# Branch B's attention values with queries on partitions, and new weave numbers

## The chip, the cores and the metric

The kernel runs on one core of a Trainium2 chip. A core has a matrix engine (PE, with its weight loads shown apart as PEld), a vector engine (DVE), a scalar engine (ACT), a general engine (POOL) and a queue that issues transfers (SP). They work side by side, each in its own program order, and wait for each other by semaphores. The metric is the device time in microseconds of one execution.

## The reference, cut to what matters

One encoder layer is applied to two groups of 1024 tokens (`prompt`, then `sample`), all in float32. Branch B is differential attention with 4 heads; each head has two 64-wide query and key maps and 128-wide values:

```python
s = jnp.einsum('bqhmd,bkhmd->bhmqk', qblk, k).astype(jnp.float32) * scale
p = jax.nn.softmax(s, axis=-1)
pd = (p[:, :, 0] - lam * p[:, :, 1]).astype(v.dtype)
return jnp.einsum('bhqk,bkhe->bqhe', pd, v)
...
ob = diff_attention(qb, kb, vb, lam)
ob = rms_norm(ob, subln_g) * (1.0 - lam_init)
ob = ob.reshape(B, S, BR_B) * jax.nn.silu(zb)
```

So each query row of a head's 128 values is divided by its root mean square, scaled by a gain, and multiplied by a gate. Then both branches are projected (`w_proj_a`, `w_proj_b`), merged by sigmoid gates and projected again.

## The kernel before, in words

Everything is kept transposed: channels on partitions, tokens along the row. A large matmul splits each float32 operand into a high and a low part of a faster 32-bit type and adds three products (the input projection in `proj_tt` L613 and `z_gen` L824, the branch projections in `merge_gen` L1097, the output projection in `out_gen` L1128). The attention values are plain float32 matmuls; the profile shows two PE records for each such instruction of the code.

**Attention.** `attention` walks a list of units. In phases 0 and 1 these are branch A's; in phases 2 to 5 a unit is one head of branch B with a pair of 128-query tiles (`pr` 0 to 3), so there are 16 B units in a group and 32 in all. For each query tile and map, `softmax_unit` makes 128x1024 scores in a two-bank PSUM tile `s` (there are two of these), takes the row maximum on DVE, and the exponential on ACT into a tile `p`. `flip` adds the second map to the first (L895), transposes `p` in 32x32 blocks on DVE (L896), and four DMAs of 128 KB put the blocks in place in a tile `q`, keys on partitions (L901, `q<-p`). `b_values` then multiplies: the value block of 128 keys is the weight that PE holds, and 256 queries stream past it, eight instructions for a unit (L953). The result `acc` in the one PSUM tile `a` has the 128 value channels on partitions and the queries along the row. It is squared by ACT (L968), copied by DVE (L969) and stored to a DRAM tile `od`. Because the channels lie on partitions, the sum of squares of a query is a sum over partitions: two float32 matmuls against a column of ones (L975), with the squares as weights. DVE collects the sums (L977, `ssB`); after the last unit of a head POOL forms the inverse roots of all 1024 queries (L980 to L983).

**Back end.** `gated_gen(i, hf)` prepares the input of the projection for two heads (`i` 2 and 3 are branch B's pairs of heads) and one half `hf` of the queries (half 0 holds units `pr` 0 and 1, half 1 holds `pr` 2 and 3). On `hf` 0 of a B pair it first turns the roots of two heads by a PE transpose (L1041), copies the rows (L1043) and stores them to a DRAM tile `rB`. Then, for each head, it loads `od` and the gate `zd`, loads the roots spread over all 128 partitions (`tab<-rB`, L1063), multiplies the three (L1064, L1068) and splits the product in two parts (L1069, L1070) in a tile `u`, which `merge_gen` uses as a moving operand (L1097).

**Order.** `weave` interleaves the streams of a phase (attention, the next head's projections, the gates' projections) by tables of weights: `Z_SHARE`, `ATT_W`, `IN_A`, `Z_A` and so on. `LAST_ATT`, `LAST_FILL`, `GATED_A` and `TAIL` do it for the stretch in which the last head's attention runs beside branch A's merge. On top of that a list scheduler sets each engine's final program order, and inside `attention` work has a higher priority. PE, DVE, ACT and POOL then run that order as it stands.

Of the kernel before, what the change touches and what calls it, by code (L numbers as in the profile page):

```python
# [37 lines left out]
    (8, 21, 4, 2, 4, 3),  # L38
    (13, 12, 5, 3, 2, 6),
)  # L40
Z_HEAD = (7, 6)
Z_HEAD_A = (-0.3, -0.32)
ATT_W = (
    (0.825, 1.067, 1.068, 1.192, 1.03, 1.769),
    (1.154, 1.862, 1.041, 1.271, 0.783, 1.144),
)
IN_A = (
    (0.32, -0.07, 0.7, 0.05, 0.25, 0.15),
    (0.1, -0.05, 0.33, 0.3, -0.03, 0.55),
)  # L50
Z_A = (
    (0.2, 0.05, 0.12, -0.05, -0.1, -0.05),
    (0.03, 0.07, 0.2, 0.15, -0.3, -0.1),
)
LAST_ATT = (47, 41)
LAST_FILL = (22, 23)
GATED_A = (0.1, -0.15)
# [4 lines left out]
FIRST_ATT = 15  # L62
FIRST_A = 0.26
TAIL = (2, 5)
TAIL_A = (1.15, 1.2)
LAG = 2
Z_FIRST = (9, 8)
Z_FIRST_A = (-0.05, -0.05)
# [4 lines left out]
BEHIND_A = 1.4  # L73
AHEAD = 100
PV_LAG = 2
A_WAIT = 1
TRAIN = 200

WHOLE = (True, True)
# [31 lines left out]
def kernel(ctx: ExitStack, tc: tile.TileContext, t: dict):  # L111
# [669 lines left out]
    def vb_gen(ht, out, pr):  # L781
        w = load_w(w_cols(w_in, (C_VB + pr * 256, 256)))
        if WHOLE[pr]:
            v = utile().bitcast(F32).rearrange("p (n h e) -> p n h e", n=NTT, h=2)
            out[2 * pr], out[2 * pr + 1] = v[:, :, 0], v[:, :, 1]
        else:
            vs = [utile().rearrange("p (n s e) -> p n s e", n=NTT, s=2) for _ in range(2)]
            out[2 * pr], out[2 * pr + 1] = vs
        for tt in range(NTT):
            ps = yield from proj_tt(ht, w, tt)  # L790
            if WHOLE[pr]:
                nc.scalar.activation(v[:, tt].rearrange("p h e -> p (h e)"), ps, AF.Copy)
                yield 1
                continue
            for i in range(2):
                vp = ps[:, i * P : (i + 1) * P]
                nc.scalar.activation(vs[i][:, tt, 0, :], vp, AF.Copy)
                nc.vector.tensor_tensor(
                    out=vs[i][:, tt, 1, :], in0=vp, in1=vs[i][:, tt, 0, :].bitcast(F32), op=ALU.subtract
                )  # L800
            yield 1
# [35 lines left out]
    def query_order(x):  # L837

        return x.rearrange("p (t i b) -> p i t b", t=2, i=4)

    def piece_order(x):
        return x.rearrange("p (i t b) -> p i t b", t=2, i=4)

    def softmax_unit(q, rs, sw, k, pt, su):


        m = tiny.tile([P, 1], F32, tag="m", name=nm("m"))
        s = sbank()
        for n in range(2):
            sl = slice(n * 512, (n + 1) * 512)  # L850
            nc.tensor.matmul(s[:, sl], q, k[:, sl], start=True, stop=False)  # L851
            nc.tensor.matmul(s[:, sl], sw, k[:, sl], start=False, stop=True)  # L852
        nc.vector.tensor_reduce(out=m, in_=s, axis=AX.X, op=ALU.max, negate=True)  # L853
        nc.scalar.activation(m, m, AF.Copy, scale=rs)
        nc.scalar.activation(  # L855
            pt.rearrange("p (j c a) -> p j c a", j=4, c=8), s.rearrange("p (c a j) -> p j c a", c=8, j=4),
            AF.Exp, scale=rs, bias=m, accum_out=su,
        )

    def scores(u, i):  # L860
# [4 lines left out]
        if "j" in u:  # L865
            qt = u["qt"]
            t = qt % 2
            softmax_unit(
                u["q"][i][:, qt * P : (qt + 1) * P], u["rs"](qt, i), u["sw"][:, i, t * P : (t + 1) * P], u["k"],
                pt, u["su"][:, i, qt : qt + 1],  # L870
            )
            u[i] = [pt]
            return i
# [3 lines left out]
        softmax_unit(u["q"][m][:, qt * P : (qt + 1) * P], u["rs"](qt, m), u["sw"][:, m, t * P : (t + 1) * P], u["k"][m], pt, su)  # L877
# [10 lines left out]

    def flip(u, t):

# [5 lines left out]
        nc.vector.transpose(pt, pt)  # L896
        if t == 0:
            u["pT"] = pair(F32R)
        dst = u["pT"].bitcast(F32).rearrange("p (i t f) -> p i t f", i=4, t=2)
        for i in range(4):  # L900
            dma(dst[:, i, t], pt[i * 32 : i * 32 + 32])  # L901

    def pT_pieces(u):

        pT = u["pT"].rearrange("p (q c b) -> p c q b", q=8, c=8)
        for cc in range(4):
            tl = pT[:, cc * 2 : cc * 2 + 2]
            th = tpool.tile([P, 2, 8, 32], F32R, tag="hi", name=nm("hi"), bufs=3)
            nc.scalar.activation(th, tl.bitcast(F32), AF.Copy)
            nc.vector.tensor_tensor(out=tl, in0=tl.bitcast(F32), in1=th.bitcast(F32), op=ALU.subtract)  # L910
            yield cc, th, tl

    def a_values(u):
        if u["qt"] % 2 == 0:
# [4 lines left out]
            x.bitcast(F32).rearrange("p (i t c b) -> p t c i b", i=4, t=2, c=8) for x in (turned["pT"], u["pT"])  # L919
# [17 lines left out]
    def b_values(u):  # L937
        acc = ps_a.tile([P, 512], F32, tag="a", name=nm("a"))[:, :256]
        ready = []
        def pv(cc, th, tl):  # L940
            for c in range(2):
                k = cc * 2 + c
                for s, rt in ((0, th), (0, tl), (1, th)):
                    nc.tensor.matmul(
                        acc, u["v"][:, k, s, :], rt[:, c, :],
                        start=(k == 0 and s == 0 and rt is th), stop=(k == 7 and s == 1),
                    )

        if WHOLE[u["h"] // 2]:
            pT = u["pT"].bitcast(F32).rearrange("p (q c b) -> p c q b", q=8, c=8)  # L950
            yield 1
            for k in range(NCH):
                nc.tensor.matmul(acc, u["v"][:, k], pT[:, k], start=(k == 0), stop=(k == 7))  # L953
                if k % 2:
                    yield 1
        else:
            for piece in pT_pieces(u):
                ready.append(piece)
                if len(ready) > PV_LAG:
                    pv(*ready.pop(0))  # L960
                yield 1
            while len(ready) > 1:
                pv(*ready.pop(0))
                yield 1
            pv(*ready.pop())
        sq = mtile("at", [P, 256], bufs=1)
        o = mtile("oo", [P, 256])
        nc.scalar.activation(query_order(sq), piece_order(acc), AF.Square)  # L968
        nc.vector.tensor_copy(query_order(o), piece_order(acc))  # L969
# [4 lines left out]
        for i in range(2):  # L974
            nc.tensor.matmul(ps[:, i : i + 1], sq[:, i * P : (i + 1) * P], ones_c, start=True, stop=True)  # L975
        ss = u["ss"][:, u["h"]]
        nc.vector.tensor_copy(ss[:, pr * 2 : pr * 2 + 2], ps[:, 0:2])  # L977
        if pr == 3:
            su = u["su"]
            nc.gpsimd.tensor_tensor(out=su, in0=su, in1=su, op=ALU.mult)  # L980
            nc.gpsimd.tensor_scalar(out=su, in0=su, scalar1=2.0 * HD * EPS, scalar2=1.0, op0=ALU.mult, op1=ALU.mult)
            nc.gpsimd.tensor_tensor(out=ss, in0=ss, in1=su, op=ALU.add)
            nc.gpsimd.tensor_tensor(out=ss, in0=ss, in1=nhalf[:, :NTT], op=ALU.pow)  # L983
        yield 1

    def attention(units, feed):
# [3 lines left out]
        for n, (ph, _, _) in enumerate(units):  # L990
            na, nv = (2, 4 + PV_LAG) if ph < 2 else (4, 5 + PV_LAG)
# [36 lines left out]
    def gated_gen(st, i, hf, oT):  # L1028
# [9 lines left out]
        if i > 1 and hf == 0:  # L1038
            ss = st["ssB"][:, 2 * i - 4 : 2 * i - 2].rearrange("p j n -> p (j n)")
            ps = fbank()[:16, :P]  # L1040
            nc.tensor.transpose(ps, ss, ident)  # L1041
            row = rtile()[:16, :P]
            nc.scalar.activation(row, ps, AF.Copy)  # L1043
            dma(st["rB"][i - 2], row)
        rA = st["rA"].rearrange("(j h n) p -> j h (n p)", j=8, h=2)
        rB = st["rB"][i % 2].rearrange("(j h n) p -> j h (n p)", j=2, h=2)
# [5 lines left out]
        for c in range(2):  # L1052
# [4 lines left out]
            rb = mtile("tab", [P, 512])  # L1057
            if e < 4:
                for a in range(2):
                    dma(rb[a * 64 : a * 64 + 64], rA[2 * e + a, hf].partition_broadcast(64))  # L1060
                nc.vector.tensor_tensor(out=o, in0=o, in1=z, op=ALU.mult)
            else:
                dma(rb, rB[e % 2, hf].partition_broadcast(P))  # L1063
                nc.vector.scalar_tensor_tensor(  # L1064
                    out=o, in0=o, scalar=subg, in1=z,
                    op0=ALU.mult, op1=ALU.mult,
                )
            nc.vector.tensor_tensor(out=o, in0=rb, in1=o, op=ALU.mult)  # L1068
# [95 lines left out]
    def new_state(g):  # L1164
        st = {"turned": False, "ht": {}, "qa": {}, "qkb": {}, "vb": {}, "zd": {}, "gad": {}, "gbd": {}, "md": {}}
        for name, n in (("suA", 8), ("suB", 4), ("ssB", 4)):
            st[name] = const.tile([P, n, NTT], F32, tag=name, name=nm(name), bufs=2 if name == "ssB" else 1)
# [3 lines left out]
        st["rB"] = [dpool.tile([16, P], F32, name=nm("rB")) for _ in range(2)]  # L1171
# [5 lines left out]
    def units_of(st):  # L1177
# [10 lines left out]
        def b_unit(h, pr):  # L1188
# [5 lines left out]
                "od": st["od"][4 + h], "ss": st["ssB"], "su": st["suB"][:, h],  # L1194
# [39 lines left out]
    for g in range(2):  # L1234
# [11 lines left out]
        def phase(k, *fs, more=()):  # L1246
            n_att = 16 * (6 + PV_LAG) - (FIRST_ATT if g == k == 0 else 0) if k < 2 else 4 * (9 + PV_LAG)
# [98 lines left out]
```

## Time and profile before

| What | Value |
|---|---|
| median of 3 runs | 1900.5 us (1896.01 to 1902.73) |
| profiled execution, first to last instruction | 1894.9 us |
| mean granted clock of PE in it | 0.993 |
| DMA moved | 299.54 MB, 158 GB/s |

The profile names no time of its own for the profiled execution beside its span; the span is 1.1 us below the fastest run shown and 5.6 us below the median. The prompt's branch B attention fills about 506 to 795 us of the span, the sample's about 1385 to 1700 us, and each is followed by the two merges and the output projection. An engine's row gives its busy time, its share of the span and its instructions. In the timeline, a row is a run of equal instructions with its start, its length from the first start to the last end, and its count; since matmuls overlap, the step from one to the next is shorter than the duration of one.

### The profile page before, as it was taken

The page shows a single profiled execution, that of the slowest core. Times are in us where ns is not written, and L with a number is a line of the kernel's source. Part 1 is how long each engine was busy: PE and PEld are TensorE (multiplying, and loading weights), DVE is VectorE, ACT ScalarE, POOL GpSimd, SP SyncE. Part 2 cuts the span into 40 slices and gives each one's busy share as a digit, 9 for nine tenths or more (in the row PEclk, how much of TensorE's full clock was granted, in tenths as well). Part 3 has the DMA queues.
Part 4 walks back from the last instruction along what each step waited for, and adds up shares of the span by engine and source line. Part 5 has one row for each costly group of instructions (what it writes and reads, how often), then busy time and mean ns, then how long its engine had stood idle before and what let it go on. Part 6 is the DMA issues. An engine that isn't in the chain of part 4 may idle for free.

```text
span 1894.9 us, 31953 instructions
## 1 busy us (share of the span) xinstructions
PE 1849.3 (98%) x11430; PEld 1590.8 (84%) x11430; DVE 1231.4 (65%) x1904; ACT 850.1 (45%) x1807; POOL 366.5 (19%) x686
## 2 busy tenths in 40 slices
PE   6899999999999999999999999999999999999999
PEld 4778888888888898787889888888888999877887
DVE  4766766455487667868365777656548776787731
ACT  3544545344455455524223455545446555552310
POOL 0442100011235241010124211000133423300000
PEclk9999999999999999999999999999999999999999
DMA  9135677664355346887551466766625344579532
GB/s 320 59 85 146 162 196 191 170 164 135 100 148 158 93 106 164 248 273 226 193 167 46 123 179 182 197 179 175 168 67 133 102 109 121 135 235 294 189 106 78
DMA packets 277628, 299.54 MB, mean 158 GB/s; under 512 B 37664, under 2 KB 228320, under 8 KB 277472
## 3 DMA queue, kind: packets, MB, share of 16 engines
q1 hardware_dynamic: 277472, 297.51, 55.5%
q8 instruction: 92, 1.51, 0.3%
q14 instruction: 64, 0.52, 0.1%
HBM read 137.91 MB, written 42.04 MB: 95 GB/s over the span
## 4 chain that ended last, share of the span: by engine, by line
PE 82%; DMA 6%; DVE 5%; SPq 3%; ACT 2%; issue 1%; POOL 0%; DVEq 0%; ACTq 0%
PE f L824 23%; PE f L613 20%; PE a L927 6%; PE f L1128 6%; PE s L851 5%; PE s L852 5%; PE a L953 4%; PE f L1097 4%; PE s L1128 3%; PE s L1097 2%; SPq L901 2%; PE s L107 1%; PE f L673 1%; DMA p<-zd 1%; DMA row<-zd 1%
## 5 line engine op out<-in xcount | busy, mean ns | idle before, releaser
L824 PE MATMUL f<-u,w 128*128 128x512 f32 x2184 | 552.9, 394 | 1.7 <-ACT w L206 0.7
L824 PEld LDWEIGHTS f<-u,w 128*128 128x128 f32 x2184 | 401.1, 188 | 81.4 <-ACT w L206 0.9
L613 PE MATMUL f<-w,u 128*128 128x256 f32 x3264 | 449.9, 286 | 2.3 <-DVE u L107 1.5
L613 PEld LDWEIGHTS f<-w,u 128*128 128x128 f32 x3264 | 425.1, 191 | 24.0 <-issue 3.8
L853 DVE TENSOR_REDUCE m<-s 128x1 f32<-128x1024 f32 x256 | 309.7, 1218 | 145.1 <-PE s L852 142.5
L896 DVE STREAM_TRANSPOSE p<-p 128x1024 f32<-128x1024 f32 x192 | 238.3, 1242 | 54.6 <-ACT p L855 49.6
L852 PE MATMUL s<-u,sw 128*128 128x512 f32 x512 | 203.1, 398 | 0.0
L207 DVE TENSOR_TENSOR w<-st,w 128x512 fp32r<-128x512 f32 x188 | 126.3, 704 | 80.8 <-ACT w L206 80.6
L206 ACT ACTIVATE w<-st 128x512 fp32r<-128x512 f32 x188 | 108.9, 625 | 143.2 <-DMA st<-in_w_in_dram 63.7
L855 ACT ACTIVATE p<-s,m,rsB 128x1024 f32<-128x1024 f32 x128 | 154.2, 1205 | 5.2 <-DVE p L895 1.6
L855 ACT ACTIVATE p<-s,m,rsA 128x1024 f32<-128x1024 f32 x128 | 154.4, 1206 | 4.0
L1097 PE MATMUL f<-u,w 128*128 128x512 f32 x576 | 142.3, 397 | 8.6 <-ACT u L1069 3.4
L638 POOL TENSOR_TENSOR rsB<-ss,nhalf 128x4 f32<-128x4 f32 x64 | 66.9, 1045 | 413.8 <-DVE ss L637 404.4
L1097 PEld LDWEIGHTS f<-u,w 128*128 128x128 f32 x576 | 108.9, 190 | 33.6 <-ACT u L1069 3.8
L953 PE MATMUL a<-q,u 128*128 128x256 f32 x512 | 124.6, 379 | 0.8 <-DMA row<-zd 0.7
L927 PE MATMUL a<-q,u 128*64 128x128 f32 x2048 | 123.6, 275 | 0.8 <-DMA q<-p 0.7
L927 PEld LDWEIGHTS a<-q,u 128*64 128x64 f32 x2048 | 112.5, 137 | 12.0 <-issue 7.0
L676 DVE TENSOR_TENSOR u<-f,u 64x256 fp32r<-64x256 f32 (+1 forms) x208 | 84.2, 407 | 50.0 <-ACT u L675 44.7
L851 PE MATMUL s<-u 128*128 128x512 f32 x256 | 109.6, 428 | 3.0 <-ACT p L855 2.9
L1128 PE MATMUL f<-u,w 128*128 128x512 f32 x480 | 111.2, 389 | 0.0
L852 PEld LDWEIGHTS s<-u,sw 128*128 128x128 f32 x512 | 97.0, 189 | 16.1
L953 PEld LDWEIGHTS a<-q,u 128*128 128x128 f32 x512 | 94.1, 190 | 15.2 <-issue 2.3
(195 smaller groups left out, 2101.2 us busy)
## 6 DMA issues: line engine op xcount, KB each, us to landing
q<-p SPq DMA_DIRECT2D x768, 128.0 KB, 2.8
st<-in_w_in_dram SPq DMA_DIRECT2D x128, 256.0 KB, 3.3
zd<-ev SPq DMA_DIRECT2D x96, 256.0 KB, 2.7
sw<-u SPq DMA_DIRECT2D x256, 64.0 KB, 2.1
p<-zd SPq DMA_DIRECT2D x64, 256.0 KB, 4.6
u<-in_w_ada_dram SPq DMA_DIRECT2D x16, 512.0 KB, 8.9
od<-oo SPq DMA_DIRECT2D x64, 128.0 KB, 2.6
st<-in_w_in_dram SPq DMA_DIRECT2D x64, 128.0 KB, 2.8
```

Of the source, the lines that this page charges most:

```text
L207: nc.vector.tensor_tensor(out=wl, in0=st, in1=wh.bitcast(F32), op=ALU.subtract)
L613: nc.tensor.matmul(ps, lt[c][:, sl], w[c][:, wi, :], start=(k == 0), stop=(k == 23))
L824: nc.tensor.matmul(ps, w[c][:, wi, e * P : (e + 1) * P], rt[c], start=(k == 0), stop=(k == 23),)
L851: nc.tensor.matmul(s[:, sl], q, k[:, sl], start=True, stop=False)
L852: nc.tensor.matmul(s[:, sl], sw, k[:, sl], start=False, stop=True)
L853: nc.vector.tensor_reduce(out=m, in_=s, axis=AX.X, op=ALU.max, negate=True)
L855: nc.scalar.activation(pt.rearrange("p (j c a) -> p j c a", j=4, c=8), s.rearrange("p (c a j) -> p j c a", c=8, j=4), AF.Exp, scale=rs, bi ...
L896: nc.vector.transpose(pt, pt)
L927: nc.tensor.matmul(acc[e * 64 : e * 64 + 64, n * P : n * P + P], u["v"](k), blocks[n][:, e, k], start=(k == 0 and n == 1), stop=(k == 7 an ...
L953: nc.tensor.matmul(acc, u["v"][:, k], pT[:, k], start=(k == 0), stop=(k == 7))
L1097: nc.tensor.matmul(ps, w[:, c, wi, d * P : (d + 1) * P], o[:, oi, :], start=(k == 0), stop=(k == 11))
L1128: nc.tensor.matmul(ps, w[c][:, wi, e * P : (e + 1) * P], m[:, mi, :], start=(k == 0), stop=(k == 23))
```

## The change

The two operands of the values' matmul change places. A block of 128 transposed probabilities (128 keys by 128 queries) is the weight, and the 128 value channels of the keys stream past it; a unit takes 16 instructions of half the length. `acc` then has queries on partitions, so a query's sum of squares is a sum along its row, which ACT forms with the square (`accum_out`). POOL makes the two inverse roots of a query at once for each unit, ACT scales the rows by them, and two PE transposes turn the 256 queries back to channels on partitions before the store to `od`. The tile `rB`, its turn, its store and its 16 spread loads go, and so does a multiply for each B head and half.

For a weight block to be addressed with one step from column to column, the exponential now writes `p` with the chunk index innermost (`by_chunks`): neighbouring keys of a 32-key run lie 8 elements (32 bytes) apart. DVE's transpose reads and writes with that step, and the weight block `pT[:, t, k]` has 128 columns 8 elements apart. Branch A keeps its order. The number tables of the weave are set anew, and code paths that were switched off are deleted.

```diff
 Z_SHARE = (
-    (8, 21, 4, 2, 4, 3),
-    (13, 12, 5, 3, 2, 6),
+    (8, 21, 4, 2, 4, 1),
+    (13, 12, 5, 3, 2, 7),
 )
...
-LAST_ATT = (47, 41)
-LAST_FILL = (22, 23)
+LAST_ATT = (41, 42)
+LAST_FILL = (22, 25)
...
-BEHIND_A = 1.4
+BEHIND_A = 1.975
...
-A_WAIT = 1
+A_WAIT = 0
...
         nc.scalar.activation(
-            pt.rearrange("p (j c a) -> p j c a", j=4, c=8), s.rearrange("p (c a j) -> p j c a", c=8, j=4),
+            pt, s.rearrange("p (c a j) -> p j c a", c=8, j=4),
             AF.Exp, scale=rs, bias=m, accum_out=su,
         )
...
+    def by_chunks(pt):
+
+        return pt.rearrange("p (j a c) -> p j c a", j=4, c=8)
...
-        nc.vector.transpose(pt, pt)
+            pb = by_chunks(pt)
+            nc.vector.transpose(pb, pb)
+        else:
+            nc.vector.transpose(pt, pt)
...
     def b_values(u):
...
-            for k in range(NCH):
-                nc.tensor.matmul(acc, u["v"][:, k], pT[:, k], start=(k == 0), stop=(k == 7))
-                if k % 2:
-                    yield 1
...
-        sq = mtile("at", [P, 256], bufs=1)
-        o = mtile("oo", [P, 256])
-        nc.scalar.activation(query_order(sq), piece_order(acc), AF.Square)
-        nc.vector.tensor_copy(query_order(o), piece_order(acc))
-        pr = u["pr"]
-        dma(u["od"][pr // 2][:, (pr % 2) * 256 : (pr % 2 + 1) * 256], o)
-        yield 1
-        ps = fbank()
-        for i in range(2):
-            nc.tensor.matmul(ps[:, i : i + 1], sq[:, i * P : (i + 1) * P], ones_c, start=True, stop=True)
-        ss = u["ss"][:, u["h"]]
-        nc.vector.tensor_copy(ss[:, pr * 2 : pr * 2 + 2], ps[:, 0:2])
-        if pr == 3:
...
+        pT = u["pT"].rearrange("p (t n c) -> p t c n", t=2, c=8)
...
+        nc.gpsimd.tensor_tensor(out=floor, in0=su[:, qs], in1=su[:, qs], op=ALU.mult)
+        nc.gpsimd.tensor_scalar(out=floor, in0=floor, scalar1=2.0 * HD * EPS, scalar2=1.0, op0=ALU.mult, op1=ALU.mult)
+        for t in range(2):
             for k in range(NCH):
+                nc.tensor.matmul(acc[:, t], pT[:, t, k], u["v"][:, k], start=(t == k == 0), stop=(t == 1 and k == 7))
+                if k % 4 == 3:
                     yield 1
+        sq = mtile("at", [P, 256], bufs=1)[:, :P]
+        nc.vector.tensor_copy(o, acc)
+        for t in range(2):
+            nc.scalar.activation(sq, o[:, t], AF.Square, accum_out=ss[:, t : t + 1])
+        nc.gpsimd.tensor_tensor(out=ss, in0=ss, in1=floor, op=ALU.add)
+        nc.gpsimd.tensor_tensor(out=rs, in0=ss, in1=nhalf[:, :2], op=ALU.pow)
         yield 1
+        for t in range(2):
+            nc.scalar.activation(o[:, t], o[:, t], AF.Copy, scale=rs[:, t : t + 1])
+        ps = fbank()[:, :256]
+        for t in range(2):
+            nc.tensor.transpose(ps[:, t * P : (t + 1) * P], o[:, t], ident)
+        oT = mtile("oT", [P, 256], bufs=1)
+        nc.vector.tensor_copy(oT, ps)
+        dma(u["od"][pr // 2][:, (pr % 2) * 256 : (pr % 2 + 1) * 256], oT)
         yield 1
...
     def gated_gen(st, i, hf, oT):
...
-        if i > 1 and hf == 0:
-            ss = st["ssB"][:, 2 * i - 4 : 2 * i - 2].rearrange("p j n -> p (j n)")
-            ps = fbank()[:16, :P]
-            nc.tensor.transpose(ps, ss, ident)
-            row = rtile()[:16, :P]
-            nc.scalar.activation(row, ps, AF.Copy)
-            dma(st["rB"][i - 2], row)
...
             else:
-                dma(rb, rB[e % 2, hf].partition_broadcast(P))
-                nc.vector.scalar_tensor_tensor(
-                    out=o, in0=o, scalar=subg, in1=z,
-                    op0=ALU.mult, op1=ALU.mult,
-                )
-            nc.vector.tensor_tensor(out=o, in0=rb, in1=o, op=ALU.mult)
+                nc.vector.scalar_tensor_tensor(out=o, in0=o, scalar=subg, in1=z, op0=ALU.mult, op1=ALU.mult)
```

The first place is ACT's program order at one B unit of the prompt. Before (its `acc` is `a_1170`; L854 turns the row maximum into a bias, L855 is the exponential, L675 splits keys or queries of the next head):

```order
L854 ACTIVATE m_1172_7733<-m_1172_7733,rsB_5_123 128x1
L675 ACTIVATE u_1034_6950<-f_1148_7627 64x2x128
L855 ACTIVATE p_1171_7732,suB_2_120<-s_1173_7734,m_1172_7733,rsB_5_123 128x1024
L854 ACTIVATE m_1177_7758<-m_1177_7758,rsB_5_123 128x1
L968 ACTIVATE at_1200_7865<-a_1170_7731 128x4x2x32
L675 ACTIVATE u_1033_6949<-f_1154_7669 64x2x128
L855 ACTIVATE p_1175_7756,su_1176_7757<-s_1178_7759,m_1177_7758,rsB_5_123 128x1024
L675 ACTIVATE u_1034_6950<-f_1154_7669 64x2x128
```

In the changed kernel a unit (`oo_1177`) stands so; L833 and L834 are the bias and the exponential, L936 the squares, L941 the scaling that needs POOL's roots `rsb`:

```order
L833 ACTIVATE m_1185_7805<-m_1185_7805,rsB_4_122 128x1
L936 ACTIVATE at_1192_7857,ssb_1174_7762<-oo_1177_7765 128x128
L834 ACTIVATE p_1183_7803,su_1184_7804<-s_1186_7806,m_1185_7805,rsB_4_122 128x4x8x32
L936 ACTIVATE at_1192_7857,ssb_1174_7762<-oo_1177_7765 128x128
L674 ACTIVATE u_1056_7068<-f_1147_7607 64x2x128
L941 ACTIVATE oo_1177_7765<-oo_1177_7765,rsb_1176_7764 128x128 x2
L833 ACTIVATE m_1190_7848<-m_1190_7848,rsB_4_122 128x1
L834 ACTIVATE p_1189_7847,suB_2_120<-s_1191_7849,m_1190_7848,rsB_4_122 128x4x8x32
```

One ACT instruction on `acc` has become four on its copy `oo`, with the next bias and exponential right behind the two that wait for POOL.

The second place is PE at the end of the prompt's attention. Before, from the last unit's squares (L975) over the turn of the roots (L1041) to the first use of `u_1376`, the gated product of the last two heads for query half 0:

```order
L975 MATMUL f_1372_8676<-ones_c_98,at_1367_8653 128x1 x2
L1097 MATMUL f_1371_8662<-u_1258_8126,w_1351_8553 128x512
L1097 MATMUL s_1402_8867<-u_1324_8425,w_1387_8770 128x512 x6
L1097 MATMUL f_1373_8684<-u_1210_7909,w_1351_8553 128x512 x6
L1097 MATMUL f_1373_8684<-u_1258_8126,w_1351_8553 128x512 x6
L1041 MATMUL f_1374_8698<-ident_93,ssB_3_121 16x128
L1097 MATMUL f_1381_8724<-u_1210_7909,w_1351_8553 128x512 x6
L1097 MATMUL f_1381_8724<-u_1258_8126,w_1351_8553 128x512 x6
L1097 MATMUL f_1394_8791<-u_1297_8288,w_1387_8770 128x512 x6
L1097 MATMUL f_1398_8829<-u_1297_8288,w_1387_8770 128x512 x6
L1097 MATMUL f_1399_8846<-u_1297_8288,w_1387_8770 128x512 x6
L1097 MATMUL f_1394_8791<-u_1376_8703,w_1387_8770 128x512
```

The same place in the changed kernel, where L944 are the last unit's transposes, L1049 the merge, `u_1428` the last heads' product for query half 0 and `u_1431` for half 1:

```order
L1049 MATMUL s_1441_9056<-u_1428_8980,w_1433_9018 128x512
L944 MATMUL f_1426_8974<-ident_93,oo_1421_8916 128x128
L1049 MATMUL s_1441_9056<-u_1428_8980,w_1433_9018 128x512
L1049 MATMUL f_1440_9039<-u_1331_8477,w_1433_9018 128x512 x6
L1049 MATMUL f_1440_9039<-u_1428_8980,w_1433_9018 128x512 x6
L1049 MATMUL s_1441_9056<-u_1428_8980,w_1433_9018 128x512 x3
L1049 MATMUL f_1444_9077<-u_1331_8477,w_1433_9018 128x512 x6
L1049 MATMUL f_1444_9077<-u_1428_8980,w_1433_9018 128x512 x6
L1049 MATMUL f_1445_9094<-u_1331_8477,w_1433_9018 128x512 x6
L1049 MATMUL f_1445_9094<-u_1428_8980,w_1433_9018 128x512 x6
L1049 MATMUL s_1448_9115<-u_1365_8628,w_1433_9018 128x512 x6
L1049 MATMUL s_1448_9115<-u_1431_9006,w_1433_9018 128x512 x3
```

Half 0 of the last heads is now used before the last unit's transposes, since it needs only units `pr` 0 and 1; half 1 comes 46 matmuls behind them, where before half 0 itself stood 49 merge matmuls behind the last unit's sums.

More of the change, by code (lines that the diff above doesn't have):

```diff
@@ L830, in z_gen @@
                 yield 1
[L837 to L842, printed above, removed]
     def softmax_unit(q, rs, sw, k, pt, su):
@@ L937, in b_values @@
     def b_values(u):
[L938 to L950, printed above, removed]
-            yield 1
+        h, pr, su = u["h"], u["pr"], u["su"]
@@ L1193, in b_unit @@
                 "rs": lambda qt, m: st["qkb"]["rs"][:, h, qt, m : m + 1],
-                "od": st["od"][4 + h], "ss": st["ssB"], "su": st["suB"][:, h],
+                "od": st["od"][4 + h], "su": st["suB"][:, h],
             }
```

103 lines of the change are left out of this document (38 added, 65 removed).

## Prediction, made before the changed kernel ran

> **What bounds the kernel now.** I read the page's totals first, then what PE waited for, then the stretches in which the change lies, then single rows for prices. The page's span, its busy row, the granted clock and the chain that ended last:
>
> ```profile
> span 1894.9 us, 31953 instructions
> PE 1849.3 (98%) x11430; PEld 1590.8 (84%) x11430; DVE 1231.4 (65%) x1904; ACT 850.1 (45%) x1807; POOL 366.5 (19%) x686
> PEclk9999999999999999999999999999999999999999
> PE 82%; DMA 6%; DVE 5%; SPq 3%; ACT 2%; issue 1%; POOL 0%; DVEq 0%; ACTq 0%
> ```
>
> PE is busy for all but 45.6 us (1894.9 - 1849.3) at an unthrottled clock, and it carries 82% of the chain. So a change is worth two things: the time that it adds to or takes from PE's own stream, and what it does to those 45.6 us. What DVE, ACT, POOL and the queue gain or lose counts only where PE waits for it. Busy per stretch (us of span, then PE, PEld, DVE, ACT, POOL); the first is the prompt's branch B attention, the second its merges and output projection:
>
> ```profile
> 506.00:795.00 289.00, 282.41 (x1665) 243.31 (x1665) 213.94 (x328) 156.37 (x340) 94.47 (x201) 0.99 0.52 143
> 795.00:900.00 105.00, 100.96 (x438) 82.41 (x437) 81.17 (x127) 35.79 (x65) 5.61 (x7) 0.97 0.79 250
> ```
>
> In branch B's attention DVE is at 74%, ACT at 54%, and PE loses 6.6 us; in the merges PE loses 4.0 us. Whom PE waited for in the two stretches that hold an end of the attention and the merges (prompt, then sample; total, times, longest):
>
> ```profile
> PE f L1097 <- ACT u L1069: 3.4, 1, 3.4
> PE f L1097 <- DVE ssB L977: 2.0, 1, 2.0
> ...
> PE f L1041 <- POOL ssB L983: 0.6, 1, 0.6
> ...
> PE f L1097 <- ACT row L1043: 1.4, 1, 1.4
> PE s L1097 <- ACT u L1069: 0.6, 1, 0.6
> ```
>
> These five, 8.0 us in all, hang on the roots: on the sums (L977), on POOL (L983), on the turned rows (L1043) and on the gated product that needs the spread roots (L1069).
>
> **The change, part by part.** Prices come from PE's timeline: start, length from first start to last end, count. The step between equal matmuls is (length - duration of one) / (count - 1), or the start of what follows less the first start, divided by the count.
>
> ```profile
> 551.97 0.38 PE L673 MATMUL f<-ident,row 128*128 128x128 f32 x2
> 552.18 1.89 PE L953 MATMUL a<-q,u 128*128 128x256 f32 x8
> ...
> 558.41 0.50 PE L975 MATMUL f<-ones_c,at 128*128 128x1 f32 x4
> 558.78 0.49 PE L851 MATMUL s<-u 128*128 128x512 f32 x1
> 559.10 0.40 PE L852 MATMUL s<-u,sw 128*128 128x512 f32 x1
> 559.34 0.40 PE L851 MATMUL s<-u 128*128 128x512 f32 x1
> ...
> 303.64 3.71 PE L927 MATMUL a<-q,u 128*64 128x128 f32 x64
> 307.28 0.50 PE L851 MATMUL s<-u,u 128*128 128x512 f32 x1
> ...
> 1007.71 4.46 PE L613 MATMUL f<-w,u 128*128 128x256 f32 x36
> ```
>
> and the mean durations (ns, after the comma) from the groups with shapes kept apart:
>
> ```profile
> L613 PE MATMUL f<-w,u 128*128 128x256 f32 x3264 | 449.9, 286 | 2.3 <-DVE u L107 1.5 <-DVE ev L808 0.6 <-DVE u L676 0.2
> L953 PE MATMUL a<-q,u 128*128 128x256 f32 x512 | 124.6, 379 | 0.8 <-DMA row<-zd 0.7
> L927 PE MATMUL a<-q,u 128*64 128x128 f32 x2048 | 123.6, 275 | 0.8 <-DMA q<-p 0.7
> ```
>
> *Values.* Before: 512 records at (1.89 - 0.379) / 7 = 0.216 us, 110.5 us. After: the same number of multiplications in 1024 records, each with 128 moving columns and a fresh weight of 128 columns. No row has that form. The nearest is branch A's L927: 128 moving columns in plain float32, and two records, side by side in the two halves of PE's columns, load 64 + 64 weight columns. It takes (307.28 - 303.64) / 64 = 0.0569 us, 0.1138 for two: 1024 x 0.1138 = 116.5 us, so +6.0 us. The ends: the same row without its hand-over to the next line, (3.71 - 0.275) / 63 x 2 = 0.109, gives +1.1; L613, which also loads 128 columns for each matmul, (4.46 - 0.286) / 35 = 0.119, gives +11.6. I take L927 since its moving operand has the same type.
>
> *Sums of squares.* 128 records of L975 leave, four for a unit. In the rows above they hold PE for 558.78 - 558.41 = 0.37 us, and the score matmul behind them steps 0.32 where 0.24 is usual: 0.45 x 32 = -14.4 us.
>
> *Turning back.* Two float32 transposes for a unit come. L673 is that form: 552.18 - 551.97 = 0.21 us for two, x 32 = +6.7 us. The four turns of L1041 go: -0.4 us at the same price.
>
> PE's stream in all: 6.0 - 14.4 + 6.7 - 0.4 = -2.1 us.
>
> *The waits for the roots.* With roots made unit by unit, the gated product of query half 0 needs only units `pr` 0 and 1 and is placed ahead of the last unit's transposes. Half 1 stands 46 merge matmuls behind them in the prompt, about 46 x 0.24 = 11.0 us, and much more in the sample. What must happen in that time: a copy (0.42, priced below), the store, the load, and three steps on 128x512 like L1070:
>
> ```profile
> od<-oo SPq DMA_DIRECT2D x64, 128.0 KB, 2.6
> ...
> q<-od SPq DMA_DIRECT2D x8, 256.0 KB, 5.5
> ```
>
> ```profile
> L1070 DVE TENSOR_TENSOR u<-q,u 128x512 fp32r<-128x512 f32 x8 | 5.3, 684 | 0.8 <-ACT u L1069 0.7
> ```
>
> That is 0.42 + 2.6 + 5.5 + 3 x 0.68 = 10.6 us, hardly less than its cover; late next is this same load. Before, the path had POOL's roots, a turn, a store and the spread load on top. I let four of the five waits go (3.4 + 0.6 + 1.4 + 0.6 = 6.0 us) and keep the one of 2.0 us: there PE waited for DVE to empty an `f` bank, and the new transposes also hold an `f` bank until DVE copies it (DVE is 77% busy there). Ends: 0 and -8.0.
>
> *Off the path.* Per unit there is now a chain from the values to the transposes, priced by these rows (copy; square and scaling of 128x128, by L634; the square's read-out; POOL's small steps, by L982; the root of two columns):
>
> ```profile
> L969 DVE COPY oo<-a 128x256 f32<-128x256 f32 x32 | 13.3, 416 | 3.6 <-ACT at L968 3.0
> L634 ACT ACTIVATE row<-row 128x128 f32<-128x128 f32 x12 | 3.7, 309 | 0.0
> L855 ACT ACTIVATION_READ_ACCUMULATOR p<-s,m,rsB 128x1 f32 x128 | 24.4, 191 | 0.0
> L982 POOL TENSOR_TENSOR ssB<-ssB,suB 128x8 f32<-128x8 f32 x8 | 2.6, 325 | 67.8 <-DVE ssB L977 67.8
> L638 POOL TENSOR_TENSOR rs<-ss,nhalf 128x2 f32<-128x2 f32 x16 | 11.5, 717 | 61.2 <-DVE ss L637 46.9 <-ACT p L633 14.0 <-PE f L824 0.2
> ```
>
> 0.42 + 2 x (0.31 + 0.19) + 0.33 + 0.72 + 2 x 0.31 = 3.1 us. In the new program order PE has between 7 and 46 us of other matmuls (counted, at the steps above) between a unit's last value matmul and its transposes, so I cost the chain at nothing; if ACT's queue ran 4 us late, the shortest cover would be gone. ACT gains 64 x (0.31 + 0.19 + 0.31) = 52 us less 32 old squares of some 0.4 (the size of L969), from 45% to 47%. POOL gains 32 x (3 x 0.33 + 0.72) = 55 us less the eight old root chains. DVE gains 32 copies (13.3 us) and loses 16 multiplies of 0.68 (10.9 us) and 32 small copies: nothing. The queue loses 16 loads of 256 KB and 4 stores. The wait that is added is ACT's, before the scaling, for POOL's add and root (1.05 us at most when POOL is free); queued behind it are the bias and the exponential, for whose emptied `s` bank PE's next scores wait. ACT idles 289 - 156 = 133 us of that stretch, so it is covered there. `A_WAIT`, `BEHIND_A` and the tables move work among streams that all keep PE fed; the 37.6 us of PE's loss that have nothing to do with roots, most of them before 150 us, I leave as they are, with 4 us to either side.
>
> *Steps of 32 bytes.* The exponential writes `p`, DVE turns it and PE loads its weights with 8 elements from one to the next. No row reads or writes SBUF so. The nearest is the exponential itself, which reads PSUM 4 elements apart, against ACT's other 128x1024 instruction, which reads and writes without gaps; and DVE's transpose is without gaps:
>
> ```profile
> L855 ACT ACTIVATE p<-s,m,rsB 128x1024 f32<-128x1024 f32 x128 | 154.2, 1205 | 5.2 <-DVE p L895 1.6 <-ACT m L854 0.2
> L566 ACT ACTIVATE s<-p 128x1024 f32<-128x1024 f32 x8 | 8.2, 1019 | 1.1 <-DVE p L1103 1.0
> L896 DVE STREAM_TRANSPOSE p<-p 128x1024 f32<-128x1024 f32 x192 | 238.3, 1242 | 54.6 <-ACT p L855 49.6
> ```
>
> A gapped read thus costs at most 1205 / 1019 = 1.18 there. I take no cost for PE: a weight column is used at 128 in 0.11 us, 1.2 a ns, hardly faster than the 0.85 a ns that ACT gets through a gapped read. The other end is the first rival.
>
> The sum is -2.1 - 6.0 = -8.1 us, on the profiled execution 1894.9 to 1886.8. Its span is 5.6 us under the median of the runs, and the same step takes the median from 1900.5 to 1892.4.
>
> **Rivals.**
>
> *Gapped weight loads are slow (slower).* Place: PEld, all 1024 loads of the values. At the 1.18 of the row above a record takes 0.1345, +21 us: 1913.6. At twice the time, 0.218, it is 1024 x 0.104 = +107 us: 1999. It decides from 8 ns a record on (8.1 us / 1024), that is above 0.122. For it: PE would be weight bound here, PEld is already 84% busy. Against it: the small slope of ACT's row. [...]
>
> *The waits come back.* Half 1's load is as long as its cover, and the `f` bank still waits for DVE. Then only PE's stream counts: 1900.5 - 2.1 = 1898.4. For it: a path of 10.6 us under a cover of 11.0. Against it: in the sample the cover is far longer.
>
> *ACT or DVE is late.* If the gapped transpose took double, DVE would have 32 x 1.24 = 40 us more in the prompt's stretch, 254 of 289 (88%). PE loses 2.3% at DVE's 74% and 3.8% in the merges at 77%; 2.5% more of the two stretches (289 and 315 us) would be 15 us: 1907. ACT's wait for POOL in front of the exponentials works the same way.
>
> **How the numbers follow.** Forecast 0.55, slow weights 0.17 (about half of it near 1914, half far above), waits back 0.18, ACT or DVE late 0.10. The predicted time is the forecast's, 1892. Its own range is 1884 to 1898: the ends of the values (-4.9, +5.6) and of the waits (-2.0, +6.0), not all at once. The whole range takes in the rivals up to the mild case of slow weights, 1914, and below the forecast's best with the 4 us of the order, 1882; outside lie the far half of slow weights (0.09) and about 0.08 of tails. A change within 0.3% (1894.8 to 1906.2), about what a measurement can tell here, counts as the same. Faster: 0.43 from the forecast and 0.04 from the waits' case, 0.47. Same: 0.12 + 0.13 and 0.03 of the others, 0.28. Slower: 0.25.
>
> **What the profile after would show.** The new value line with 1024 records at a step of 0.109 to 0.119 us; 0.2 us for a pair of turns; no L975; ACT near 890 us busy; no PE wait of over 1 us for a gated product or a row of roots; the transpose and the exponential of branch B within 5% of 1.24 and 1.21 us. A value step above 0.122, a B transpose near 2 us, or PE waits on the new transposes or on exponentials of 10 us in sum would make the prediction wrong.

## The result: 5.8% slower, and the profile after

The changed kernel took 2008.6 us (median of 4 runs, 2005.6 to 2011.3) beside 1899.9 us of the kernel before: ratio 1.0576, 95% interval 1.0556 to 1.0596. The forecast was 1892 us, its range ended at 1914. Of the profile after, the span and busy rows and the chain by engine:

```profile
span 2005.3 us, 33049 instructions
PE 1964.3 (98%) x11874; PEld 1724.7 (86%) x11874; DVE 1287.3 (64%) x1888; ACT 1005.3 (50%) x1963; POOL 394.3 (20%) x782
PE 86%; DVE 5%; ACT 3%; issue 2%; DMA 2%; POOL 1%; SPq 1%; DVEq 0%; POOLq 0%; ACTq 0%
```

The span grew by 110.4 us, and PE's busy time by 115.0 (1964.3 - 1849.3). PE's idle time is 41.0 us where it was 45.6. So in sum PE waits no longer, though for other things (5.7 us for POOL's rows before L672, where it was 0.4, and none for the roots): PE's own stream got longer. DVE has 56 us more and ACT 155 us, though ACT was to gain some 40. The groups of branch B's values (L930), exponential (L834, `rsB`) and transpose (L882), with branch A's transpose (L884) and exponential (L834, `rsA`), which the change leaves alone; after the bar busy us, mean ns, idle before:

```profile
L834 ACT ACTIVATE p<-s,m,rsB 128x1024 f32<-128x1024 f32 x128 | 294.4, 2300 | 3.9 <-DMA q<-p 0.5
L834 ACT ACTIVATE p<-s,m,rsA 128x1024 f32<-128x1024 f32 x128 | 154.5, 1207 | 4.0 <-ACT m L833 0.2
L882 DVE STREAM_TRANSPOSE p<-p 128x1024 f32<-128x1024 f32 x64 | 139.1, 2173 | 0.9
L884 DVE STREAM_TRANSPOSE p<-p 128x1024 f32<-128x1024 f32 x128 | 158.9, 1243 | 58.8 <-ACT p L834 55.7
L930 PE MATMUL a<-u,q 128*128 128x128 f32 x1024 | 257.9, 391 | 1.2 <-DMA q<-p 1.1
L944 PE MATMUL f<-ident,oo 128*128 128x128 f32 x64 | 12.9, 273 | 0.3 <-DVE u L675 0.3
```

Each pair holds the answer side by side: the same exponential, with the same number of elements and the same read, takes 2.30 us where it writes with gaps of 32 bytes and 1.21 without; the transpose 2.17 and 1.24. PE's timeline shows the third:

```profile
660.86 0.38 PE L672 MATMUL f<-ident,row 128*128 128x128 f32 x2
661.07 3.97 PE L930 MATMUL a<-u,q 128*128 128x128 f32 x16
664.80 0.47 PE L830 MATMUL s<-u 128*128 128x512 f32 x1
```

A value record steps (3.97 - 0.391) / 15 = 0.239 us, where 0.114 was forecast. The loads of its weights are what got longer; their rows in this kernel and, below, in the run `flat_both`, where the weight columns lie side by side:

```profile
L930 PEld LDWEIGHTS a<-u,q 128*128 128x128 f32 x1024 | 256.6, 331 | 5.4 <-DMA q<-p 1.6
...
L930 PEld LDWEIGHTS a<-u,q 128*128 128x128 f32 x1024 | 141.0, 193 | 22.0 <-DMA q<-p 9.1
```

Summed over the whole trace from each start to the start of what follows (idle gaps left out), the values went from 97.0 to 221.3 us, the sums from 12.1 to 0 and the turns from 0 to 5.8: +118, near the 115.0 of PE's busy time. (In such a sum the last record of a run counts short, since the next instruction starts early; so it gives 97.0 where 512 steps of 0.216 us give 110.5.)

The waits for the roots are gone. In the two stretches where they were, the waits for the work of branch B's end are now these (prompt's merges, then the sample's):

```profile
PE s L830 <- ACT p L834: 1.3, 1, 1.3
PE a L930 <- DMA q<-p: 1.1, 1, 1.1
...
PE s L830 <- ACT p L834: 1.8, 1, 1.8
```

None hangs on a root, where 8.0 us did.

### The profile page after: what moved, and what is told of

Read it like the earlier page. It is cut to its first block, busy times and chain, and to the rows that moved or that the text cites. A ratio compares the mean times of both kernels' runs of the same rounds, so it can differ in the third digit from the quotient of the medians.

```text
span 2005.3 us, 33049 instructions
## 1 busy us (share of the span) xinstructions
PE 1964.3 (98%) x11874; PEld 1724.7 (86%) x11874; DVE 1287.3 (64%) x1888; ACT 1005.3 (50%) x1963; POOL 394.3 (20%) x782
## 4 chain that ended last, share of the span: by engine, by line
PE 86%; DVE 5%; ACT 3%; issue 2%; DMA 2%; POOL 1%; SPq 1%; DVEq 0%; POOLq 0%; ACTq 0%
PE f L810 22%; PE f L612 17%; PE a L930 10%; PE f L1049 7%; PE a L905 6%; PE f L1080 5%; PE s L830 5%; PE s L831 5%; PE s L1080 3%; PE s L1049 2%; ACT p L834 2%; PE s L106 1%; DVE p L882 1%; SPq L889 1%; PE f L672 1%
## 5 line engine op out<-in xcount | busy, mean ns | idle before, releaser
L810 PE MATMUL f<-u,w 128*128 128x512 f32 x2160 | 547.5, 394 | 0.7 <-ACT w L205 0.7
L810 PEld LDWEIGHTS f<-u,w 128*128 128x128 f32 x2160 | 395.2, 188 | 77.1 <-ACT w L205 0.9
L834 ACT ACTIVATE p<-s,m,rsB 128x1024 f32<-128x1024 f32 x128 | 294.4, 2300 | 3.9 <-DMA q<-p 0.5
L930 PEld LDWEIGHTS a<-u,q 128*128 128x128 f32 x1024 | 256.6, 331 | 5.4 <-DMA q<-p 1.6
L930 PE MATMUL a<-u,q 128*128 128x128 f32 x1024 | 257.9, 391 | 1.2 <-DMA q<-p 1.1
L884 DVE STREAM_TRANSPOSE p<-p 128x1024 f32<-128x1024 f32 x128 | 158.9, 1243 | 58.8 <-ACT p L834 55.7
L205 ACT ACTIVATE w<-st 128x512 fp32r<-128x512 f32 x188 | 109.9, 627 | 131.5 <-DMA st<-in_w_in_dram 53.4
L834 ACT ACTIVATE p<-s,m,rsA 128x1024 f32<-128x1024 f32 x128 | 154.5, 1207 | 4.0 <-ACT m L833 0.2
L882 DVE STREAM_TRANSPOSE p<-p 128x1024 f32<-128x1024 f32 x64 | 139.1, 2173 | 0.9
L1049 PE MATMUL f<-u,w 128*128 128x512 f32 x576 | 138.2, 391 | 0.0
L1049 PEld LDWEIGHTS f<-u,w 128*128 128x128 f32 x576 | 107.6, 188 | 21.9
L675 DVE TENSOR_TENSOR u<-f,u 64x256 fp32r<-64x256 f32 (+1 forms) x210 | 84.6, 406 | 63.6 <-ACT u L674 58.3
L1080 PE MATMUL f<-u,w 128*128 128x512 f32 x480 | 111.2, 389 | 0.0
```

The source lines that it names most:

```text
L810: nc.tensor.matmul(ps, w[c][:, wi, e * P : (e + 1) * P], rt[c], start=(k == 0), stop=(k == 23),)
L834: nc.scalar.activation(pt, s.rearrange("p (c a j) -> p j c a", c=8, j=4), AF.Exp, scale=rs, bias=m, accum_out=su,)
L882: nc.vector.transpose(pb, pb)
L930: nc.tensor.matmul(acc[:, t], pT[:, t, k], u["v"][:, k], start=(t == k == 0), stop=(t == 1 and k == 7))
L1049: nc.tensor.matmul(ps, w[:, c, wi, d * P : (d + 1) * P], o[:, oi, :], start=(k == 0), stop=(k == 11))
L1080: nc.tensor.matmul(ps, w[c][:, wi, e * P : (e + 1) * P], m[:, mi, :], start=(k == 0), stop=(k == 23))
```

## The experiments

Three explanations had to be told apart: that PE's gapped weight loads alone make the loss; that the exponential and the transpose, about 1 us longer each, hold PE up; and that matmuls of 128 columns with a weight of their own are slow, gaps or not.

**The weights without gaps** (`flat_weights`).

```
-        pT = u["pT"].rearrange("p (t n c) -> p t c n", t=2, c=8)
+        pT = u["pT"].rearrange("p (t c n) -> p t c n", t=2, c=8)
```

> The changed kernel, but each weight block of the values is 128 neighbouring columns of the same tile instead of 128 columns 32 bytes apart. It pairs probabilities with the wrong keys, so only its times are read; the exponential and DVE's transpose still write and read with the 32-byte step. Theory 1 (the weight load pays for the step): the values' step goes from 0.238 us a record back to about 0.114 and the time falls by 1024 x 0.124 = 127 us, to 1880 to 1890. Theory 2 (a plain float32 weight of 128 columns can't be loaded beside a matmul of 128 moving columns, whatever its step): the step stays at 0.238 and the time at 2008. Theory 3 (the slower exponential and transpose, 2.30 and 2.17 us, hold PE up): both stay.

Measured: 1977.4 us, 1.0412 [1.0395, 1.043]. Its busy row, the values' group and PE's longest waits (total, times, longest):

```profile
PE 1881.2 (95%) x11874; PEld 1617.7 (82%) x11874; DVE 1285.6 (65%) x1888; ACT 996.6 (50%) x1963; POOL 390.7 (20%) x782
...
L930 PE MATMUL a<-u,q 128*128 128x128 f32 x1024 | 157.0, 284 | 20.9 <-DMA q<-p 15.3
```

```profile
PE s L830 <- ACT p L834: 24.7, 31, 1.9
PE a L930 <- DMA q<-p: 15.3, 17, 4.0
...
PE a L930 <- DVE oo L934: 4.0, 3, 2.2
```

The step fell to 0.112 us, and yet only 31 us came back. PE now waits for the exponential that empties its `s` bank and for turned weights that come late: the slow weight loads had hidden an ACT and a DVE that were slow as well. That PE's weights alone make the loss falls here.

**`p` without gaps, the weights still with them** (`flat_p`): `by_chunks`, through which exponential and transpose see `p`.

```
-        return pt.rearrange("p (j a c) -> p j c a", j=4, c=8)
+        return pt.rearrange("p (j c a) -> p j c a", j=4, c=8)
```

> The changed kernel with the exponential and DVE's transpose of branch B without gaps, as before the change, and the weight blocks still read with the 32-byte step (again the wrong keys, so only its times are read). Theory 1: exponential back to 1.21 us and transpose to 1.24, some 140 us less of ACT and 60 us less of DVE, and yet the time stays within 5 us of 2008, since PE's stream is the same. Theory 2: the same. Theory 3: the time falls by most of the 109 us.

Measured: 1995.7 us, 1.051 [1.0494, 1.0526]. Exponential and transpose are back at 1204 and 1240 ns; PE is busy 1961.5 of 1993.5 us:

```profile
L930 PE MATMUL a<-u,q 128*128 128x128 f32 x1024 | 257.7, 391 | 0.0
```

**Both without gaps** (`flat_both`, the two edits together).

> Both: no gaps for ACT, DVE or PE (wrong keys, only its times are read). It holds every part of the change but the 32-byte step. Theory 1, with the terms of the prediction (values +6, sums -14.4, turns +6.7, waits -6): 1885 to 1895, within 5 us of the run that only has flat weights. Theory 2: about 2008. Theory 3: about 1890, and clearly below the run that only has flat weights.

Measured: 1895.6 us (10 runs, 1894.6 to 1901.9), 0.9991 [0.9981, 1.0001]. Its busy row, a row of its timeline, and three of PE's waits (the first and the last are not in the kernel before; the second, for DVE to empty a bank in branch A's merge, stood there with 1.6 us):

```profile
PE 1850.1 (98%) x11874; PEld 1604.3 (85%) x11874; DVE 1229.9 (65%) x1888; ACT 878.2 (46%) x1963; POOL 393.0 (21%) x782
...
617.76 1.95 PE L930 MATMUL a<-u,q 128*128 128x128 f32 x16
```

```profile
PE a L930 <- DMA q<-p: 6.5, 6, 4.0
...
PE f L1049 <- DVE u L1060: 2.3, 1, 2.3
...
PE f L672 <- DVE oT L946: 1.6, 1, 1.6
```

The gaps are the whole loss: without them the change costs nothing. The step is (1.95 - 0.279) / 15 = 0.111 us, so 128 columns with a weight of their own aren't slow. Against flat_both, gapped weights cost 100.1 us, gapped exponential and transpose 81.8, and both together 113.0, not 181.9. They are two bounds side by side: a PE slowed by its weights gives ACT and DVE the time they need (it waits 4.9 us for the exponential in the changed kernel, 24.7 in flat_weights). Undoing either one leaves most of the loss standing.

**The step that decides, for weights** (`step_ladder`): 1, 2, 4 and 8 elements in the four `pr` (L933, L935, L937, L939), the rest as after.

```
+        step = (1, 2, 4, 8)[pr]
+        pT = u["pT"].rearrange("p (t g n s) -> p t g s n", t=2, s=step, n=P)
```

> The changed kernel; the weight columns are 1, 2, 4 and 8 elements (4, 8, 16, 32 bytes) apart in the units of query pairs 0, 1, 2 and 3, each on a line of its own (wrong keys but for the last, only its times are read). Theory 1: 0.114 us a record at 1, 0.238 at 8; if what matters is that two columns lie in the same 16 bytes, 0.114 at 2 and 0.238 at 4; if the price grows with the distance, values between. Theory 2: 0.238 on all four lines.

Measured in one execution; the timeline's rows, in the order of the steps:

```profile
808.95 1.27 PE L933 MATMUL a<-u,q 128*128 128x128 f32 x10
...
829.80 1.57 PE L935 MATMUL a<-u,q 128*128 128x128 f32 x12
...
655.45 6.85 PE L937 MATMUL a<-u,q 128*128 128x128 f32 x28
...
709.64 3.02 PE L939 MATMUL a<-u,q 128*128 128x128 f32 x12
```

With mean durations of 0.283, 0.292, 0.393 and 0.393 us these are (length - duration) / (count - 1) = 0.110, 0.116, 0.239 and 0.239 us. Two columns to 16 bytes cost 5%, one to 16 bytes more than doubles the time (a factor of 2.2), and a step of 32 bytes is no worse than one of 16. No step between 8 and 16 bytes was run, so it is not shown where between them the time rises.

**Which of ACT and DVE** (`exp_gap` and `transpose_gap`): weights flat, and only the exponential, or only the transpose, goes through `by_chunks`.

```
exp_gap:        -            pb = by_chunks(pt)
                -            nc.vector.transpose(pb, pb)
                +        nc.vector.transpose(pt, pt)
transpose_gap:  -            by_chunks(pt), su,
                +            pt.rearrange("p (j c a) -> p j c a", j=4, c=8), su,
```

> Like the run with flat weights, but of the two other gapped steps only the exponential keeps its 32-byte step; DVE's transpose reads and writes without gaps (wrong keys, only its times are read). With flat weights the time was 1977.4 us, with nothing gapped 1895.6, so 82 us hang on ACT or DVE. Theory A (ACT: 128 exponentials of 2.30 instead of 1.20 us, 140 us, which also hold a score bank longer): about 1965 to 1977 here. Theory B (DVE: 64 transposes of 2.18 instead of 1.24 us, 60 us, on the engine that is 74% busy there): about 1900 to 1910 here.

> The other half: flat weights, exponential without gaps, only DVE's transpose keeps the 32-byte step (wrong keys, only its times are read). Theory A: 1896 to 1910. Theory B: 1960 to 1977. If each takes a share that the other then hides, both runs lie between and their rises over 1895.6 add up to less or more than 82 us.

Measured: 1942.9 us, 1.0225 [1.0209, 1.024], and 1934.5 us, 1.0183 [1.0163, 1.0203]. PE's waits, first with the gapped exponential, then with the gapped transpose:

```profile
PE s L830 <- ACT p L834: 23.2, 30, 2.0
...
PE a L927 <- DMA q<-p: 9.2, 11, 4.0
```

```profile
PE a L930 <- DMA q<-p: 21.0, 20, 4.0
...
PE s L830 <- ACT p L834: 3.2, 4, 1.8
```

Over flat_both these are +47.3 and +38.9 us; their sum of 86.2 is near the 81.8 of both together. Neither alone is the cause. They reach PE by two doors: the exponential through the `s` bank that it empties late, the transpose through the weights that arrive late, at L930, from the loads that its end releases.

**The new numbers** (`old_numbers`): flat_both with the tables of numbers of the kernel before.

> The run with nothing gapped, with the weave's tables of numbers from before the change (wrong keys, only its times are read). If the new numbers do no more than fit the new instructions, as the prediction took it: 1890 to 1902, within 6 us of 1895.6. If the near equality with the time before (1899.1) comes from new numbers that pay for a dearer stream: 1905 or more. If the new numbers were set for a machine without the penalty of the gaps and suit this one badly: under 1890.

Measured: 1903.4 us (10 runs), 1.0022 [1.0008, 1.0037], between what the two theories asked for. Against flat_both the new numbers are worth 0.3%, some 6 to 8 us, about what can be told. With the old ones the change without gaps is slower than the kernel before by 0.2%, and in the profiled execution this is waiting more than a dearer stream: PE is busy for 1852.0 us (1849.3 before) and idle for 53.4 (45.6 before). The wait for the exponential's bank shows it, 0.7 us in flat_both:

```profile
PE s L831 <- ACT p L835: 9.6, 5, 2.7
PE a L931 <- DMA q<-p: 6.3, 8, 1.7
```

**Can the change be had without gaps of 16 bytes?** Two versions compute all that the reference does. `step_two` lays the chunks in pairs, so that keys used one after the other are 8 bytes apart, two to 16 bytes, and its loads move runs of 256 bytes instead of 1 KB:

```
-        return pt.rearrange("p (j a c) -> p j c a", j=4, c=8)
+        return pt.rearrange("p (j h a s) -> p j h s a", j=4, h=4, s=2)
...
+            dst = u["pT"].rearrange("p (t h i f) -> p i t h f", i=4, t=2, h=4)
...
-                nc.tensor.matmul(acc[:, t], pT[:, t, k], u["v"][:, k], start=(t == k == 0), stop=(t == 1 and k == 7))
+                nc.tensor.matmul(acc[:, t], pT[:, t, k // 2, k % 2], u["v"][:, k], start=(t == k == 0), stop=(t == 1 and k == 7))
```

`step_one` has no gaps at all on the engines, and its loads scatter in runs of 128 bytes:

```
+            dst = u["pT"].rearrange("p (t c i b) -> p i t c b", i=4, t=2, c=8)
```

> [...] Nothing is left out. By the ladder (0.118 us at 2 elements against 0.111 at 1) the weights cost 7 us more than without gaps. [...] If ACT and DVE pay for any gap: exponential near 2.3 us, and a time as with flat weights, 1975. If the small runs make the DMAs late: PE waits for q of 10 us and more in sum.

> The changed kernel with no gap anywhere, nothing left out: p as before the change, weight columns side by side, and the DMAs behind the transpose write runs of 128 bytes (a kilobyte in the changed kernel, 256 bytes in the run with a step of 2). Weights 0.111 instead of 0.118 us a record: 7 us less than that run, 1896 (between 1892 and 1900), about level with the kernel before, if the small runs are hidden. If they are not: landing of q<-p clearly over 2.9 us, PE waits for q over 15 us in sum, and a time of 1910 or more.

Measured: step_two 1902.8 us (10 runs), 1.0021 [1.0009, 1.0034]; step_one 1956.6 us, 1.0297 [1.0281, 1.0313]. The groups and a row of the timeline of step_two, then PE's main waits in step_one:

```profile
L834 ACT ACTIVATE p<-s,m,rsB 128x1024 f32<-128x1024 f32 x128 | 163.9, 1280 | 4.6 <-DVE p L880 1.0
...
L935 PE MATMUL a<-u,q 128*128 128x128 f32 x1024 | 146.3, 283 | 6.5 <-DMA q<-p 4.7
...
602.29 2.04 PE L935 MATMUL a<-u,q 128*128 128x128 f32 x16
```

```profile
PE a L935 <- DMA q<-p: 27.1, 19, 3.2
...
PE s L830 <- ACT p L834: 6.6, 6, 1.7
PE s L1054 <- DVE u L1065: 4.4, 1, 4.4
```

Pairs take away nearly the whole loss: 106 us of it are gone, with an exponential 6% longer and a value step of 0.118 us (the median of all records; (2.04 - 0.283) / 15 = 0.117 in the row). Yet the interval lies above 1: no form of the change that was run and computes what the reference does was faster than the kernel before. With no gaps the price moves to the loads. From issue to landing (least, median, most), for those of step_two and then step_one:

```profile
DMA to landing us min/median/max: 2.8/3.2/7.1
```

```profile
DMA to landing us min/median/max: 3.2/3.9/7.7
```

Branch A's loads, unchanged in runs of 1 KB, land in 2.8 us in both. Of step_one's loss the waits for `q` are the largest wait, but its PE idles 83.2 us (1947.3 - 1864.1) against 42.8 in flat_both, and the rest was not traced to a cause.

**Would the order before have paid as well?** (`moving_ladder`): the kernel before, whose values are the weights and whose `p` is the moving operand, with steps of 1, 2, 4 and 8 by `pr` for exponential, transpose and matmul.

```
+            step = (1, 2, 4, 8)[u["pr"]]
+            pT = u["pT"].bitcast(F32).rearrange("p (g n s) -> p g s n", s=step, n=256)
```

> The kernel before the change, values still the weights; in branch B the exponential's writes, DVE's transpose and now the moving operand have steps of 1, 2, 4 and 8 elements in the units of query pairs 0 to 3, each on a line of its own (moved blocks hold the wrong keys, only its times are read). [...] If the moving side has room (0.84 ns a column against 0.87 ns for a weight column, so no more room than there), unchanged is unlikely; unchanged would say that the penalty is one of the weight load alone.

Measured in one execution. The moving operand's median steps, over all records that follow one of the same line without a wait, are 0.216, 0.227, 0.451 and 0.460 us for 256 columns. A row for each of the steps 1, 2, 4 and 8:

```profile
613.10 1.89 PE L984 MATMUL a<-q,u 128*128 128x256 f32 x8
...
553.77 1.97 PE L986 MATMUL a<-q,u 128*128 128x256 f32 x8
...
849.72 6.04 PE L988 MATMUL a<-q,u 128*128 128x256 f32 x13
...
590.90 5.74 PE L990 MATMUL a<-q,u 128*128 128x256 f32 x12
```

With mean durations of 0.381, 0.388, 0.627 and 0.638 us these rows give 0.216, 0.226, 0.451 and 0.464 us. The groups with shapes kept apart, ACT for 1, 2, 4, 8 and then DVE for 1, 2, 4, 8:

```profile
L856 ACT ACTIVATE p<-s,m,rsB 128x1024 f32<-128x1024 f32 x32 | 38.6, 1206 | 0.9
L861 ACT ACTIVATE p<-s,m,rsB 128x1024 f32<-128x1024 f32 x32 | 41.1, 1284 | 0.9
L866 ACT ACTIVATE p<-s,m,rsB 128x1024 f32<-128x1024 f32 x32 | 70.6, 2207 | 1.0
L871 ACT ACTIVATE p<-s,m,rsB 128x1024 f32<-128x1024 f32 x32 | 73.8, 2310 | 2.3 <-DMA q<-p 0.9 <-DVE p L911 0.6
...
L923 DVE STREAM_TRANSPOSE p<-p 128x1024 f32<-128x1024 f32 x16 | 19.8, 1240 | 0.2
L915 DVE STREAM_TRANSPOSE p<-p 128x1024 f32<-128x1024 f32 x16 | 19.9, 1242 | 0.3
L918 DVE STREAM_TRANSPOSE p<-p 128x1024 f32<-128x1024 f32 x16 | 33.0, 2061 | 0.2
L921 DVE STREAM_TRANSPOSE p<-p 128x1024 f32<-128x1024 f32 x16 | 34.9, 2179 | 0.3
```

The same cliff lies between 8 and 16 bytes for PE's moving operand (0.227 and 0.451 us), ACT's writes (1.28 and 2.21 us) and DVE's transposes (1.24 and 2.06 us). It is found at every access of SBUF that was tried, not at PE's weights alone; DVE's transpose reads and writes in the same steps, so which of the two pays was not separated. The transpose took 2.01 and 2.13 ns a column in steps of 4 and 8 for 1.21 without gaps; in steps of 2 no two words that follow each other are adjacent, and yet it kept its rate (1242 / 1024 = 1.21 ns a column).

## Why the prediction was wrong, point by point

**The step that failed** is "Steps of 32 bytes", with its "I take no cost for PE". It was priced by ACT's gapped read of PSUM (1.18 at most), the only large gapped row there was; but the three new accesses go to SBUF, where the step of 32 bytes costs a factor of 2.2 for weights, 1.9 for ACT's write and 1.75 for the transpose. The row was near in kind and far in place. The text then turned the 1.18 into nothing by comparing elements a nanosecond of two engines, which says nothing on what a gap costs either of them. The first rival pointed the right way and was given 0.17. Its price of twice the time was its author's estimate, shown by no row of before; the runs showed 0.239 us a record with the step of 32 bytes and 0.111 without. The prediction's own signs of being wrong came, a value step above 0.122 us (0.239) and a transpose near 2 us (2.17).

**The rival that came true** is "Gapped weight loads are slow", at its far end: 1024 x (0.239 - 0.114) = +128 us on the values. Its price of 1999 us is near that of the weights alone, which measured 1995.7, but in part by luck: it took 0.104 us more for a record where 0.125 came, while PE's busy time rose by only 111.4 us over flat_both (1961.5 - 1850.1) and its idle time fell by 10.8 (42.8 - 32.0). "ACT or DVE is late" was true as well, and too small: 15 us were forecast for the transpose by itself, which cost 38.9, and the exponential, which gained more (128 x 1.1 = 140 us of ACT), was not priced. Behind the slow weights the two of them add only 13 us (2008.6 - 1995.7). The rivals were put as one or the other; they held at once.

**The other terms,** read in flat_both and after:
- Values: 0.111 us without gaps for a forecast of 0.114, so 1024 x 0.111 - 110.5 = +3.2 us instead of +6.0; summed from start to start, where they went from 97.0 to 104.9 us, +7.9. Branch A's row was a good price for the form.
- Sums and turns, summed in the same way: 12.1 and 5.6 us, for 14.4 and 6.7. The 14.4 held 2.6 us (0.08 x 32) for the matmul behind the sums, which this way of summing doesn't show. PE is busy for 1850.1 us in flat_both, +0.8 where -2.1 was forecast.
- The waits for the roots: all five are gone, the one of 2.0 us that I kept too. But waits of 8.1 us for late weights and for the bank of the turned values stand in their place (6.5 + 1.6). PE's idle time is 42.8 us, where 45.6 - 6.0 = 39.6 was forecast.
- So flat_both lies 3.5 us under the kernel before, where the sum said 8.1. With an interval up to 1.0001 even that can't be told from none.
- The chain of the scalings stayed off the path but for 0.7 us: so long PE waited in flat_both for ACT's scaling before the transposes of L944 (in the changed kernel not at all). ACT at 878 us without gaps fits the forecast of 890.

**What stays open.** Of gapped `p` with flat weights (+84.5 us between the profiled executions), 53 us are idle PE (96.2 against 42.8) and the rest is longer busy time of the same instructions; the granted clock in the prompt's attention was 0.97 there against 0.99 in flat_both. How much of the rest is the clock and how much the modelled ends of matmuls was not separated.

## What to carry to other kernels

Before a layout with gaps, ask at PE, ACT and DVE, where they touch it, whether float32 elements used one after the other lie at most 8 bytes apart; where they lie 16 or 32 apart, price each such instruction at about twice its time (1.7 to 2.2 times here), and price all the engines together, since undoing one of several parallel bounds gives little back (31 or 13 of 113 us here). A layout in pairs had nearly all that the full interleave was for: loads in runs of 256 bytes and engines at 94% or more of their speed; even so it was no gain over the kernel before. And a price for SBUF is not taken from a row that reads PSUM, however alike the two look (1.18 at most for ACT's gapped read of PSUM, 1.9 for its gapped write to SBUF).

## What the hardware showed that was not expected

- The cost of a step in SBUF is a cliff, not a slope: up to 8 bytes 0 to 6.5%, at 16 bytes 1.7 to 2.2 times the time, and 0 to 6% more at 32 (weights 0.110, 0.116, 0.239, 0.239 us; moving 0.216, 0.227, 0.451, 0.460; transpose 1.24, 1.24, 2.06, 2.18).
- A write pays as well: the same exponential is 1.21, 1.28, 2.21 and 2.31 us, by the step of its output alone.
- A reshuffling load of 128 KB lands in 2.8 us with runs of 1 KB, 3.2 with 256 bytes and 3.9 with 128, medians of the traces; from 256 to 128 bytes PE's waits for it went from 4.7 to 27.1 us.
